# Joining the state's two products per sub-block into one 128-column product in a chunked RWKV-7 recurrence

## The chip, the cores and the metric

The kernel runs on one core of a Trainium2 chip. The metric is device time of the whole program, in microseconds (us). The core's engines are TensorE (PE, matrix products; PEld is its weight load), VectorE (DVE), ScalarE (ACT), GpSimd (POOL) and SyncE (SP, which issues most of the DMAs). Each engine works through its own list of instructions in order; semaphores tie the lists together.

## What is computed

One pre-norm residual layer over 256 tokens of width 2048. A combined input projection (2048 x 22672, float32) feeds four token mixers; their outputs are gated, projected, merged and projected once more. The mixer that matters here is RWKV-7 time mixing, with 16 heads of 64:

```python
def step(state, inp):
    r_t, w_t, k_t, v_t, a_t, b_t = inp
    sa = jnp.einsum('bhvk,bhk->bhv', state, a_t)
    state = (state * w_t[:, :, None, :] + sa[..., None] * b_t[:, :, None, :]
             + v_t[..., None] * k_t[:, :, None, :])
    return state, jnp.einsum('bhvk,bhk->bhv', state, r_t)
...
u = jnp.einsum('bsd,dn->bsn', h, w_in)
a_in, b_in, b_gate, c_qkv, c_f, c_gate, d_in, d_gate, m_logit = _split(u, IN_SIZES)
y_a = _short_conv_branch(a_in, conv_w)
y_b = _rwkv7_branch(b_in, b_gate, ...)
y_c = _fox_branch(c_qkv, c_f, c_gate, fox_bf)
y_d = _pool_branch(d_in, d_gate, pool_w, pool_scale)
...
proj = jnp.einsum('bskc,kcd->bskd', ys, w_branch)
gates = jax.nn.sigmoid(m_logit.reshape(bsz, s, N_BRANCH, d) + b_merge)
return x + jnp.einsum('bsd,de->bse', jnp.sum(gates * proj, axis=2), w_out)
```

## The kernel before

**The big products.** All weights come from HBM in float32. `chunk` (L255) makes 512 output columns for both blocks of 128 tokens. A weight tile `raw` (two slices of 128 rows) is split by ACT into a rounded part `wh` (L275) and by DVE into the rest `wl` (L276), and PE multiplies high by high and high by low (L245, the tile written is `psm`) and low by high (L249). There are three buffers of `raw`, six of `wh` and six of `wl`, so that DVE can be at most three pairs of `wl` ahead of PE. Each pair of slices gives twelve products with 512 moving columns.

**The recurrence.** It runs for two halves of eight heads (`hf`), in each for two blocks of 128 tokens (`rwkv_block`, b = 0 and 1), in each for two sub-blocks of 64 tokens (e = 0 and 1): eight sub-blocks, of which the first of each half has no state yet (`ch` = 0). A block first transposes its scaled factors into `GT` and `BK` (L499 to L503), then the Gram matrices on PE (L509), copied under a mask into `G` by DVE (L513); four transposes (L523) bring the triangles together in `MT`, a chain of 31 small multiply and reduce steps on DVE inverts them (L530, L532), four more transposes write `UF` (L538), and L540 to L555 complete it. Then, for each sub-block:

- `from_state_and_keys(0)`: four products of the state `SB` with a 66-column slice of `GT` (L571) and eight of the tokens' values with 66-column slices of `G` (L575) are added up in the PSUM tile `ps_z`; ACT copies them to `z` (L580);
- `UF` times `z` (L584), copied by ACT into the values `uv` (L585); the state's update (L590);
- `from_state_and_keys(1)`: the same twelve products with the other 66 columns, and ACT copies them to `y` (L591; `y` is the tile that rows name `e`);
- DVE takes the update over into `SB` (L597 to L600); after the second sub-block, DVE normalises `y` (L607 to L623).

There is one buffer of `ps_z`, so the second group of products can't start before `z` has been copied.

**Order.** The tile framework orders each engine's list by a simulated timeline with priorities: the weights' split first, then the recurrence, then the attention heads (L686 to L714), then the rest. So the recurrence's instructions stand among the big products of other parts of the layer, and a change in one place moves others.

Of the kernel before, what the change touches and what calls it, by code (L numbers as in the profile page):

```python
# [9 lines left out]
F32 = mybir.dt.float32  # L10
# [3 lines left out]
ALU = mybir.AluOpType  # L14
# [80 lines left out]
def kernel(  # L95
# [267 lines left out]

    Gt = rw.tile([P, NH * 2 * P + 8], F32, name="G")
    G = slots(Gt, NH)
# [112 lines left out]
    def rwkv_block(hf, b, u, prep):  # L478
# [15 lines left out]
        for p2 in range(0, NPAIR, 2):  # L494
# [16 lines left out]
            for par in range(2):  # L511
                h = 2 * p2 + par
                v.copy_predicated(out=G[:, h:h + 3:2],  # L513
                                  mask=rmask.unsqueeze(1).unsqueeze(1).to_broadcast([P, 2, 2, P]),
                                  data=gps[par].rearrange("p (h e t) -> p h e t", h=2, e=2))
# [3 lines left out]
        for q in range(4):  # L519
            e, d = q // 2, q % 2  # L520
            ds = slice(32 * d, 32 * d + 32)
            src = G[ds, :, e, ds].rearrange("p u t -> p t u").unsqueeze(2).to_broadcast([32, 32, 4, NH])
            v.transpose(out=MT[32 * q:32 * q + 32].rearrange("p t (r u) -> p t r u", u=NH), in_=src)  # L523
# [19 lines left out]
        for h in range(NH):  # L543
            for e in range(2):
                j = (h * 2 + e) * 32
                nc.tensor.matmul(tps[0:32, j:j + 32], lhsT=G[0:32, h, e, 32:64], rhs=X1[0:32, h, e, :],
                                 start=True, stop=True)
# [14 lines left out]
        for e in range(2):  # L562
# [3 lines left out]
            def from_state_and_keys(part):  # L566

                o = psum_ex("z")
                if ch:
                    for p in range(NPAIR):  # L570
                        nc.tensor.matmul(o[0:MORE, p * P:(p + 1) * P], lhsT=after(GTt, 4 * p + 2 * e + part),  # L571
                                         rhs=SB[:, p, :], start=p == 0, stop=False)
                for h in range(NH):
                    hs = slice(h * H, (h + 1) * H)
                    nc.tensor.matmul(o[0:MORE, hs], lhsT=after(Gt, 4 * h + 2 * e + part), rhs=uv[:, hs],  # L575
                                     start=ch == 0, stop=ch == 0 or h == NH - 1)
                return o[lo]


            sc.activation(out=z[lo], in_=from_state_and_keys(0), func=AF.Copy)  # L580
# [10 lines left out]
            sc.activation(out=y[ts], in_=from_state_and_keys(1), func=AF.Copy)  # L591
# [367 lines left out]
```

## Time and profile before

| | |
|---|---|
| three runs | 1418.52, 1424.03 and 1423.12 us, median 1423.12 us |
| the profiled execution | 1420.26 us, span of the trace 1418.5 us |
| PE busy | 1387.2 us (98% of the span) |
| DVE busy | 968.3 us (68%) |
| ACT busy | 712.3 us (50%) |
| DMA | 266.20 MB, 188 GB/s on average |

The span is the time from the first to the last instruction of the trace; around it lie 1.8 us of the execution's time. A product with float32 operands shows as two PE instructions in the trace (a transpose as one), and as one row in the order of the program.

### The profile page before, as it was taken

What the parts mean: (1) busy time and instruction counts of PE and PEld (TensorE: products, weight loads), DVE (VectorE), ACT (ScalarE), POOL (GpSimd) and SP (SyncE); (2) the same over time, 40 slices, a digit from 0 to 9 for tenths busy, and PEclk for the clock granted to TensorE, in tenths of its full rate; (3) what the DMA queues carried; (4) which work ended last, traced back from release to release, by engine and by line L of the source; (5) the groups of instructions that cost most, each with busy time, mean ns of one, the idle gap of its engine ahead of it and who ended that gap; (6) DMA issues with size and microseconds to landing.
All of it is one profiled execution on the core that took longest, in us unless ns stands there. A gap on an engine that the chain in (4) does not pass through costs nothing.

```text
span 1418.5 us, 20184 instructions
## 1 busy us (share of the span) xinstructions
PE 1387.2 (98%) x6961; PEld 1149.7 (81%) x6961; DVE 968.3 (68%) x1724; ACT 712.3 (50%) x1298; POOL 75.1 (5%) x149
## 2 busy tenths in 40 slices
PE   8999999999999999999999999999999999999997
PEld 6877778887788788887888888888888888888885
DVE  5558989589857979679957655565655556556654
ACT  6455744554445565554535544444444444444444
POOL 0310000011002100010000000000000000000000
PEclk9999999999999999999999999999999999999999
DMA  7876645446557655555545566666666666776664
GB/s 243 214 214 206 189 144 177 140 129 206 177 151 221 209 162 167 175 156 166 178 147 162 161 204 198 203 192 209 203 200 187 206 209 198 231 230 201 194 201 148
DMA packets 136918, 266.20 MB, mean 188 GB/s; under 512 B 11609, under 2 KB 16392, under 8 KB 136816
## 3 DMA queue, kind: packets, MB, share of 16 engines
q1 hardware_dynamic: 128448, 239.83, 55.2%
q0 software_dynamic: 7760, 24.04, 6.1%
q8 instruction: 54, 0.88, 0.3%
q10 hardware_dynamic: 608, 1.06, 0.2%
q14 instruction: 48, 0.39, 0.1%
HBM read 257.44 MB, written 2.10 MB: 183 GB/s over the span
## 4 chain that ended last, share of the span: by engine, by line
PE 79%; DVE 6%; issue 3%; DMA 2%; ACT 1%; POOL 0%; DVEq 0%; ACTq 0%; POOLq 0%
PE psm L245 47%; PE psm L249 24%; DVE wl L276 2%; DMA raw<-in_w_out_dram 1%; PE ps_z L575 1%; PE ps_r L509 1%; DMA cg<-pz 1%; DVE MT L523 1%; DVE tm L530 1%; PE ps_z L571 1%; PE ps_c L846 1%; PE ps_r L584 0%; PE ps_c L686 0%; PE ps_r L499 0%; PE ps_c L691 0%
## 5 line engine op out<-in xcount | busy, mean ns | idle before, releaser
L276 DVE TENSOR_TENSOR wl<-raw,wh 128x512 fp32r<-128x512 f32 (+1 forms) x896 | 576.6, 679 | 334.6 <-ACT wh L275 287.1
L275 ACT ACTIVATE wh<-raw 128x512 fp32r<-128x512 f32 (+1 forms) x896 | 513.5, 619 | 542.7 <-PE psm L245 319.4
L245 PE MATMUL psm<-wh,xh 128*128 128x512 f32 (+1 forms) x1440 | 564.7, 393 | 5.5 <-ACT wh L275 3.8
L245 PE MATMUL psm<-wh,xl 128*128 128x512 f32 (+1 forms) x1440 | 560.9, 391 | 0.0
L249 PE MATMUL psm<-wl,xh 128*128 128x512 f32 (+1 forms) x1440 | 411.8, 392 | 4.3 <-DVE wl L276 4.2
L245 PEld LDWEIGHTS psm<-wh,xh 128*128 128x128 f32 x1440 | 271.3, 189 | 64.3 <-ACT wh L275 7.2
L249 PEld LDWEIGHTS psm<-wl,xh 128*128 128x128 f32 x1440 | 266.5, 188 | 62.6 <-DVE wl L276 9.7
L245 PEld LDWEIGHTS psm<-wh,xl 128*128 128x128 f32 x1440 | 271.4, 189 | 52.4 <-issue 0.5
L530 DVE TENSOR_TENSOR tm<-UQ,MT 128x16 f32<-128x16 f32 (+30 forms) x124 | 52.4, 422 | 2.1
L532 DVE TENSOR_REDUCE UQ<-tm 128x8 f32<-128x16 f32 (+30 forms) x124 | 36.2, 292 | 2.3
L782 DVE SCALAR_TENSOR_TENSOR qa<-psm,rstd,row 128x512 f32<-128x512 f32 x32 | 23.9, 748 | 18.3 <-PE psm L249 18.3
L784 ACT ACTIVATE qa<-qa 128x1024 f32<-128x1024 f32 x16 | 17.0, 1061 | 37.3 <-DVE qa L782 37.3
L184 POOL DMA_DIRECT2D row<-in_b_merge_dram x16 | 8.7, 541 | 507.0 <-DVE qa L782 433.7
L523 DVE STREAM_TRANSPOSE MT<-G 32x1024 f32<-32x1024 f32 x16 | 32.0, 2001 | 0.2
L245 PE MATMUL psm<-wh,ybh 128*128 128x512 f32 x64 | 24.9, 389 | 0.0
L245 PE MATMUL psm<-wh,ych 128*128 128x512 f32 x64 | 24.9, 389 | 0.0
L245 PE MATMUL psm<-wh,ydh 128*128 128x512 f32 x64 | 24.9, 389 | 0.0
L245 PE MATMUL psm<-wh,yah 128*128 128x512 f32 x64 | 24.9, 389 | 0.0
L245 PE MATMUL psm<-wh,yal 128*128 128x512 f32 x64 | 24.9, 389 | 0.0
L245 PE MATMUL psm<-wh,ybl 128*128 128x512 f32 x64 | 24.9, 389 | 0.0
L245 PE MATMUL psm<-wh,ycl 128*128 128x512 f32 x64 | 24.9, 389 | 0.0
L245 PE MATMUL psm<-wh,ydl 128*128 128x512 f32 x64 | 24.9, 389 | 0.0
(381 smaller groups left out, 1355.5 us busy)
## 6 DMA issues: line engine op xcount, KB each, us to landing
raw<-in_w_in_dram SPq DMA_DIRECT2D x343, 512.0 KB, 4.2
raw<-in_w_branch_dram SPq DMA_DIRECT2D x64, 512.0 KB, 4.7
raw<-in_w_out_dram SPq DMA_DIRECT2D x32, 512.0 KB, 4.9
row<-in_b_merge_dram POOLq DMA_DIRECT2D x16, 256.0 KB, 4.0
raw<-in_w_in_dram SPq DMA_DIRECT2D x8, 328.0 KB, 4.5
raw<-in_w_in_dram SPq DMA_DIRECT2D x8, 312.0 KB, 3.3
cg<-pz POOLq DMA_DIRECT2D x4, 448.0 KB, 5.3
x<-in_x_dram SPq DMA_DIRECT2D x3, 512.0 KB, 8.7
```

Of the source, the lines that this page charges most:

```text
L245: nc.tensor.matmul(ps[b][:, :n], lhsT=st[:, k, b * P:(b + 1) * P], rhs=wh[:, :n], start=k == 0 and st is sth, stop=False)
L249: nc.tensor.matmul(ps[b][:, :n], lhsT=sth[:, k, b * P:(b + 1) * P], rhs=wl[:, :n], start=False, stop=k == nk - 1)
L275: sc.activation(out=h[:, :n], in_=raw[:, j, :n], func=AF.Copy)
L276: v.tensor_tensor(out=l[:, :n], in0=raw[:, j, :n], in1=h[:, :n].bitcast(F32), op=ALU.subtract)
L509: nc.tensor.matmul(gps[par][:, j * P:(j + 1) * P], lhsT=BK[:, i, par, e, :], rhs=GT[:, p2 + i, e, :], start=True, stop=True)
L523: v.transpose(out=MT[32 * q:32 * q + 32].rearrange("p t (r u) -> p t r u", u=NH), in_=src)
L530: v.tensor_tensor(out=tm[:, :, 0:n], in0=UQ[:, i:32, :].rearrange("p j c -> p c j"), in1=MT[:, i:32, i].unsqueeze(1).to_broadcast([P, 8, n ...
L532: v.tensor_reduce(out=UQ[:, i, :], in_=tm[:, :, 0:n], axis=AX.X, op=ALU.add)
L571: nc.tensor.matmul(o[0:MORE, p * P:(p + 1) * P], lhsT=after(GTt, 4 * p + 2 * e + part), rhs=SB[:, p, :], start=p == 0, stop=False)
L575: nc.tensor.matmul(o[0:MORE, hs], lhsT=after(Gt, 4 * h + 2 * e + part), rhs=uv[:, hs], start=ch == 0, stop=ch == 0 or h == NH - 1)
L782: v.scalar_tensor_tensor(out=gt[:, b, :], in0=ps[b], scalar=rstd[:, b:b + 1], in1=bm, op0=ALU.mult, op1=ALU.add)
L784: sc.activation(out=flat(gt), in_=flat(gt), func=AF.Sigmoid)
```

## The change

The state's product is made once per sub-block, with all 128 columns of `GT`: rows 0 to 63 of `ps_z` get the share of `z`, rows 64 to 127 the share of `y`. The tokens' first eight products still have 66 columns, the last two of them zero (`G` now holds 66 columns for each slot, 64 of them written). Since they no longer cover all rows, a product of two columns with weights that are all zero closes the accumulation. ACT copies the upper half into `y` behind the copy of `z`; the tokens' eight products for `y` go to the next `ps_z` alone, and DVE adds them to `y` in place of ACT's copy. For `ch` = 0 there is no state product and ACT copies as before. The masked copy into `G` becomes two copies of half the size each.

```diff
--- before.py
+++ after.py
@@ -361,8 +361,9 @@
 
         return t[:, 0:t.shape[-1] - 8].rearrange("p (u e t) -> p u e t", u=n, e=2)
 
-    Gt = rw.tile([P, NH * 2 * P + 8], F32, name="G")
-    G = slots(Gt, NH)
+
+    Gt = rw.tile([P, NH * 2 * 2 * MORE], F32, name="G")
+    G = Gt.rearrange("p (u e w t) -> p u e w t", u=NH, e=2, w=2)
     SB = rw.tile([P, NPAIR, P], F32, name="SB")
     UFt = rw.tile([MORE, NH * 2 * SUB + 8], F32, name="UF")
     UF = slots(UFt, NH)[0:64]
@@ -510,16 +511,18 @@
                                      start=True, stop=True)
             for par in range(2):
                 h = 2 * p2 + par
-                v.copy_predicated(out=G[:, h:h + 3:2],
-                                  mask=rmask.unsqueeze(1).unsqueeze(1).to_broadcast([P, 2, 2, P]),
-                                  data=gps[par].rearrange("p (h e t) -> p h e t", h=2, e=2))
+                for w in range(2):
+                    v.copy_predicated(
+                        out=G[:, h:h + 3:2, :, w, 0:SUB],
+                        mask=rmask[:, w * SUB:(w + 1) * SUB].unsqueeze(1).unsqueeze(1).to_broadcast([P, 2, 2, SUB]),
+                        data=gps[par].rearrange("p (h e w t) -> p h e w t", h=2, e=2, w=2)[:, :, :, w])
 
 
         MT = rw.tile([P, 32, 32], F32, name="MT")
         for q in range(4):
             e, d = q // 2, q % 2
             ds = slice(32 * d, 32 * d + 32)
-            src = G[ds, :, e, ds].rearrange("p u t -> p t u").unsqueeze(2).to_broadcast([32, 32, 4, NH])
+            src = G[ds, :, e, 0, ds].rearrange("p u t -> p t u").unsqueeze(2).to_broadcast([32, 32, 4, NH])
             v.transpose(out=MT[32 * q:32 * q + 32].rearrange("p t (r u) -> p t r u", u=NH), in_=src)
         gp.memset(flat(MT)[:, 0:1024:33], 1.0)
         UQ = rw.tile([P, 32, 8], F32, name="UQ")
@@ -543,7 +546,7 @@
         for h in range(NH):
             for e in range(2):
                 j = (h * 2 + e) * 32
-                nc.tensor.matmul(tps[0:32, j:j + 32], lhsT=G[0:32, h, e, 32:64], rhs=X1[0:32, h, e, :],
+                nc.tensor.matmul(tps[0:32, j:j + 32], lhsT=G[0:32, h, e, 0, 32:64], rhs=X1[0:32, h, e, :],
                                  start=True, stop=True)
         v.tensor_copy(out=X1[32:64].rearrange("p u e t -> p (u e t)"), in_=tps[0:32, :])
         tps = psum_ex("r")
@@ -563,21 +566,24 @@
             ch = 2 * b + e
             ts = slice(e * SUB, (e + 1) * SUB)
             uv = vs[:, b, :] if e == 0 else uv1
-            def from_state_and_keys(part):
-
-                o = psum_ex("z")
-                if ch:
-                    for p in range(NPAIR):
-                        nc.tensor.matmul(o[0:MORE, p * P:(p + 1) * P], lhsT=after(GTt, 4 * p + 2 * e + part),
-                                         rhs=SB[:, p, :], start=p == 0, stop=False)
+            def from_keys(o, w, fresh):
                 for h in range(NH):
                     hs = slice(h * H, (h + 1) * H)
-                    nc.tensor.matmul(o[0:MORE, hs], lhsT=after(Gt, 4 * h + 2 * e + part), rhs=uv[:, hs],
-                                     start=ch == 0, stop=ch == 0 or h == NH - 1)
-                return o[lo]
-
-
-            sc.activation(out=z[lo], in_=from_state_and_keys(0), func=AF.Copy)
+                    nc.tensor.matmul(o[0:MORE, hs], lhsT=G[:, h, e, w], rhs=uv[:, hs], start=fresh, stop=fresh)
+
+
+            zy = psum_ex("z")
+            if ch:
+                for p in range(NPAIR):
+                    nc.tensor.matmul(zy[:, p * P:(p + 1) * P], lhsT=GT[:, p, e, :], rhs=SB[:, p, :], start=p == 0,
+                                     stop=False)
+            from_keys(zy, 0, ch == 0)
+            if ch:
+
+                nc.tensor.matmul(zy[:, HALF - 2:HALF], lhsT=K("cmask")[:, 0:P], rhs=SB[:, 0, 0:2], start=False, stop=True)
+            sc.activation(out=z[lo], in_=zy[lo], func=AF.Copy)
+            if ch:
+                sc.activation(out=y[ts], in_=zy[hi], func=AF.Copy)
             ups = psum_ex("r")
             for h in range(NH):
                 hs = slice(h * H, (h + 1) * H)
@@ -588,7 +594,12 @@
                 for p in range(NPAIR):
                     pc = slice(p * P, (p + 1) * P)
                     nc.tensor.matmul(sps[:, pc], lhsT=(bk1 if e else bk0)[:, pc], rhs=uv[:, pc], start=True, stop=True)
-            sc.activation(out=y[ts], in_=from_state_and_keys(1), func=AF.Copy)
+            yk = psum_ex("z")
+            from_keys(yk, 1, True)
+            if ch:
+                v.tensor_tensor(out=y[ts], in0=yk[lo], in1=y[ts], op=ALU.add)
+            else:
+                sc.activation(out=y[ts], in_=yk[lo], func=AF.Copy)
             if ch < NSUB - 1:
                 sv = sps.rearrange("p (a d) -> p a d", d=P)
                 for rs in (lo, hi):
```

Three places of the order show what moves. The first is PE's list at the second sub-block of the first block (half 1), `ps_z` with the state `SB` and the tokens' values `e_...`, then the attention head's products (`ps_c`) and the big ones (`psm`). Before:

```order
L571 MATMUL ps_z<-SB,GT 66x128 x4
L575 MATMUL ps_z<-e_1699,G 66x64 x8
L709 MATMUL ps_c<-va,pT 128x64
L710 MATMUL ps_c<-va,pT 128x64
L711 MATMUL ps_c<-va,pT 128x64
L686 MATMUL ps_c<-cst,qa 66x128 x2
L686 MATMUL ps_c<-cst,ka 66x128 x2
L249 MATMUL psm<-wl,xh 128x512 x4
```

And now:

```order
L578 MATMUL ps_z<-SB,GT 128x128 x4
L572 MATMUL ps_z<-e_1703,G 66x64 x8
L583 MATMUL ps_z<-SB,cst 128x2
L715 MATMUL ps_c<-cst,pt 128x128 x3
L249 MATMUL psm<-wl,xh 128x512 x4
```

The four state products have 128 rows out in place of 66, the two-column product (L583) stands behind the tokens' eight, and another step of the attention head follows. The second group of four (before, eighteen rows further down) is gone.

The second place is DVE's list in the second block of half 1, at the end of the inversion (`tm`, `UQ`), where `UF` is written. `ya` and `yc` are other mixers' outputs, `wl` is the weights' split. Before:

```order
L530 TENSOR_TENSOR tm<-UQ,MT 128x256
L532 TENSOR_REDUCE UQ<-tm 128x8
L538 STREAM_TRANSPOSE UF<-UQ 32x8x4x8
L276 TENSOR_TENSOR wl<-raw,wh 128x512
L538 STREAM_TRANSPOSE UF<-UQ 32x8x4x8 x3
L276 TENSOR_TENSOR wl<-raw,wh 128x512
L310 SCALAR_TENSOR_TENSOR ya<-psm,rstd,ya 128x512 x2
L540 STREAM_TRANSPOSE X_1966<-UF 32x512
L714 SCALAR_TENSOR_TENSOR yc<-ps_c,sm,yc 128x64 x2
L312 TENSOR_TENSOR ya<-ya,sg 128x512 x2
L276 TENSOR_TENSOR wl<-raw,wh 128x512 x6
```

And now:

```order
L276 TENSOR_TENSOR wl<-raw,wh 128x512 x2
L535 TENSOR_REDUCE UQ<-tm 128x8
L310 SCALAR_TENSOR_TENSOR ya<-psm,rstd,ya 128x512 x2
L533 TENSOR_TENSOR tm<-UQ,MT 128x256
L725 SCALAR_TENSOR_TENSOR yc<-ps_c,sm,yc 128x64 x2
L312 TENSOR_TENSOR ya<-ya,sg 128x512 x2
L535 TENSOR_REDUCE UQ<-tm 128x8
L541 STREAM_TRANSPOSE UF<-UQ 32x8x4x8 x4
L276 TENSOR_TENSOR wl<-raw,wh 128x512 x2
L543 STREAM_TRANSPOSE X_1972<-UF 32x512
L276 TENSOR_TENSOR wl<-raw,wh 128x512 x6
```

The four transposes into `UF` and the six instructions on `ya` and `yc` now stand in one piece between two pairs of `wl`, where before two single `wl` stood among them.

The third place is DVE's list in the first block of half 1, from the masked copies into `G` to the start of the inversion. Before:

```order
L513 COPY_PREDICATED G<-cst,ps_r 128x2x256 x2
L523 STREAM_TRANSPOSE MT<-G 32x1024 x3
L276 TENSOR_TENSOR wl<-raw,wh 128x512
L523 STREAM_TRANSPOSE MT<-G 32x1024
L276 TENSOR_TENSOR wl<-raw,wh 128x512 x3
L530 TENSOR_TENSOR tm<-UQ,MT 128x8x2
```

And now:

```order
L515 COPY_PREDICATED G<-cst,ps_r 128x2x2x64 x4
L526 STREAM_TRANSPOSE MT<-G 32x1024 x4
L276 TENSOR_TENSOR wl<-raw,wh 128x512 x4
L533 TENSOR_TENSOR tm<-UQ,MT 128x8x2
L276 TENSOR_TENSOR wl<-raw,wh 128x512 x2
L535 TENSOR_REDUCE UQ<-tm 128x8
```

Two copies have become four, and the single `wl` among the transposes has moved behind them.

## Rows read from the trace of the kernel before

**Rows 1.** The page: busy us (share of the span) xinstructions, and PE's granted clock in 40 slices.

```profile
PE 1387.2 (98%) x6961; PEld 1149.7 (81%) x6961; DVE 968.3 (68%) x1724; ACT 712.3 (50%) x1298; POOL 75.1 (5%) x149
...
PEclk9999999999999999999999999999999999999999
```

**Rows 2.** Waits of PE: engine line <- what ended it: us in total, times, longest us.

```profile
PE psm L249 <- DVE wl L276: 4.2, 5, 2.3
PE psm L245 <- ACT wh L275: 3.8, 5, 1.3
```

**Rows 3.** Timeline of PE, a sub-block: start us, us, engine, line, out<-in, shapes, count.

```profile
262.26 0.84 PE L249 MATMUL psm<-wl,xh 128*128 128x512 f32 x3
262.94 1.05 PE L590 MATMUL ps_r<-s,pv 128*128 128x128 f32 x8
263.83 1.12 PE L575 MATMUL ps_z<-s,G 128*66 128x64 f32 x16
...
269.94 1.03 PE L571 MATMUL ps_z<-SB,GT 128*66 128x128 f32 x8
270.81 1.12 PE L575 MATMUL ps_z<-e,G 128*66 128x64 f32 x16
```

**Rows 4.** Timeline of PE, products with few moving columns.

```profile
102.15 0.38 PE L658 MATMUL ps_c<-cf,cst 128*128 128x16 f32 x2
102.38 0.72 PE L249 MATMUL psm<-wl,xh 128*128 128x512 f32 x2
...
245.00 1.19 PE L546 MATMUL ps_r<-X,G 32*32 32x32 f32 x32
246.13 0.43 PE L709 MATMUL ps_c<-va,pT 128*128 128x64 f32 x2
```

**Rows 5.** ACT's copies out of `ps_z`, line L591: ns min/median/max, first and last start.

```profile
L591 ACT ACTIVATE e<-ps_z x8: 589/590/592, 265.0 to 747.0; 64x512 f32<-64x512 f32 x8
```

**Rows 6.** DVE by line and form: busy us, mean ns, then idle us before.

```profile
L523 DVE STREAM_TRANSPOSE MT<-G 32x1024 f32<-32x1024 f32 x16 | 32.0, 2001 | 0.2
...
L513 DVE COPY_PREDICATED G<-cst,ps_r 128x512 f32<-128x512 int32 x16 | 11.9, 741 | 6.8 <-PE ps_r L509 6.1
...
L864 DVE TENSOR_TENSOR va<-psm,qa 128x512 f32<-128x512 f32 x8 | 5.5, 683 | 0.0
...
L842 DVE COPY sg<-ps_c 128x256 f32<-128x256 f32 x8 | 3.2, 412 | 1.1 <-PE ps_c L841 1.0
```

**Rows 7.** Timeline of PE, three waits: in brackets idle us and what ended it.

```profile
372.44 0.50 PE L249 MATMUL psm<-wl,xh 128*128 128x512 f32 x1 [0.66 <-DVE wl L276]
375.23 0.50 PE L249 MATMUL psm<-wl,xh 128*128 128x512 f32 x1 [2.29 <-DVE wl L276]
...
656.28 0.33 PE L704 MATMUL ps_c<-cst,pt 128*128 128x128 f32 x1 [2.37 <-ACT pt L699]
```

**Rows 8.** Timeline of DVE around the longest wait.

```profile
372.42 2.03 DVE L538 STREAM_TRANSPOSE UF<-UQ 32x256 f32<-32x256 f32 x3
374.48 0.69 DVE L276 TENSOR_TENSOR wl<-raw,wh 128x512 fp32r<-128x512 f32 x1
375.09 1.40 DVE L310 SCALAR_TENSOR_TENSOR ya<-psm,rstd,ya 128x512 f32<-128x512 f32 x2
...
377.03 0.42 DVE L714 SCALAR_TENSOR_TENSOR yc<-ps_c,sm,yc 128x64 f32<-128x64 f32 x2
377.39 1.27 DVE L312 TENSOR_TENSOR ya<-ya,sg 128x512 f32<-128x512 f32 x2
```

**Rows 9.** Stretches behind two waits: busy us (x) of PE, PEld, DVE, ACT, POOL, granted clock.

```profile
375.70:379.10 3.40, 3.24 (x9) 2.53 (x9) 3.22 (x8) 1.26 (x2) 0.00 (x0) 0.51 0.53 154
656.90:660.30 3.40, 3.40 (x17) 2.81 (x18) 3.40 (x10) 2.68 (x5) 0.00 (x0) 1.00 0.65 166
```

**Rows 10.** The page's groups of the inversion: busy us, mean ns of one.

```profile
L530 DVE TENSOR_TENSOR tm<-UQ,MT 128x16 f32<-128x16 f32 (+30 forms) x124 | 52.4, 422 | 2.1
L532 DVE TENSOR_REDUCE UQ<-tm 128x8 f32<-128x16 f32 (+30 forms) x124 | 36.2, 292 | 2.3
```

## The prediction

> **What bounds the kernel now.** I read the page first: PE is busy for 98% of the span, DVE for 68%, and the granted clock is at nine tenths or more in all 40 slices [rows 1]. So the kernel is as long as PE's list, plus the few microseconds in which PE waits. The list of PE's waits comes next: what it waits for behind the start is the weights' split, with 4.2 us for `wl` and 3.8 us for `wh` [rows 2]. PE's timeline then says where: 0.66 and 2.29 us in the second block of half 1, and 2.37 us in the last block of half 0, for an attention tile that comes late from ACT [rows 7]. DVE's timeline shows why: at 372 to 378 us it has no gap, PE's product starts within 0.1 us of the end of the `wl` that it needs, and that `wl` stood behind three transposes of 2.03 us together [rows 7, 8]. So in the four blocks DVE lags behind PE for a while, because the inversion's 248 small steps (52.4 and 36.2 us) and the transposes stand among the splits [rows 10]. The change thus has two prices: what it takes from PE's list, and what it does to DVE's lag.
>
> **PE's list.** The state products of six sub-blocks are made once in place of twice: 6 x 4 = 24 of 48 go. Four of them hold PE from 269.94 to 270.81 us, 0.87 us or 0.218 each [rows 3]; 24 are 5.2 us. Those that stay load 128 columns of weights in place of 66. The nearest row with such weights and the same 128 moving columns is the state's update: four from 262.94 to 263.83 us, 0.222 each [rows 3]; 24 x 0.004 is 0.1 us.
>
> Added are six closing products of two moving columns. The trace has none so narrow; two rows lie near. Products with 32 moving columns and 32 x 32 weights take 16 in 1.13 us, 0.07 each; one with 16 moving columns, but 128 x 128 weights, holds PE from 102.15 to 102.38 us, 0.22 with the step to the next form [rows 4]. So a product of eight times fewer moving columns than the state's costs the same where its weights are as wide: the weights set it. I take 0.22, which has the same weights: 1.3 us, with 0.4 us as the other end. The Trainium skill says so too (TensorE: Matmul & The Clock Gate, section LDWEIGHTS): the load's time goes by the columns of the stationary operand, not by its rows, 128 columns being 107 ns by its formula; for two passes that would be an estimate of 0.21 each, in agreement with the 0.22 here, and it speaks against the change, since counting moving columns alone would make the closing product nearly free.
>
> The sixteen products with the tokens per sub-block stay at 66 columns and 64 moving ones: nothing. PE's list: -5.2 + 0.1 + 1.3 = -3.8 us (-4.7 with the cheap closing product).
>
> **ACT.** Six copies to `y` go and six of the same form come, 0.59 us each [rows 5]: nothing in sum. The new one stands behind the copy of `z` and so ahead of the copy to `uv`, but that one waits for eight products (L584) of the form of L575's eight, which take 1.12 us [rows 3]; 0.59 us is hidden there. The single `ps_z` is free again only when it is done, which matters for the tokens' second products; in the order these follow the closing product by 37 big products in the first block, 8 us at 0.227 each [rows 3].
>
> **DVE.** Sixteen masked copies of 0.741 us become 32 of half the size. The nearest form is a copy of 128x256 from PSUM, 0.412 us [rows 6]: 2 x 0.412 - 0.741 = +0.08 a pair, 1.3 us in all, 0.3 us a block; if the split costs nothing, 0, and if every half cost the whole 0.741, 11.9 us (I take the copy's row, which has the size). By the fixed cost per instruction that the skill's VectorE: DVE Perf Modes gives for sources in PSUM (section on the TRN2 errata, 120 cycles at 0.96 GHz, 125 ns) it would be an estimate of 2.0 us; no row here has the split copy. Six additions of 64x512 come, at the 0.683 us of an addition out of PSUM [rows 6]: 4.1 us. The transposes that read `G` at its new stride stay at 2.0 us each [rows 6]; with none at such a stride in the trace I leave +-10%, 0.8 us a block. As DVE is idle for a third of the span, these 5.4 us cost only where PE waits on DVE: within the blocks. An addition also holds `ps_z`, but in the order the next user of that tile stands 16 or more big products, 3.6 us, behind, against about 1.5 us for the state's instructions and the addition ahead of it.
>
> **DVE's lag, the uncertain term.** The order of the whole middle has moved. At the second place shown, DVE now has in one piece between two pairs of `wl`: 1.40 (`ya`), 0.42 (`yc`), 1.27 (`ya`) and 4 x 0.68 (transposes, a third of 2.03), with one multiply and two reduces at their means about 6.8 us [rows 8, 10], where the longest such piece there was before 3.4 us. A pair of slices is twelve big products, 2.7 us on PE [rows 3], so PE runs dry. On the other hand the two `wl` on which it waited before now come ahead of this piece. At the third place the piece grows from 2 x 0.74 + 3 x 2.0 = 7.5 us to 4 x 0.41 + 4 x 2.0 = 9.6 us [rows 6], though the last transpose was only one `wl` behind before.
>
> To weigh it I added up, from each block's last Gram product on, the durations of the rows over DVE's order up to each `wl` and over PE's up to its first use, and took the largest excess of DVE over PE. Before it is 1.9, 4.9, 0.6 and 3.7 us for the four blocks, 11.1 in sum; now 2.7, 6.5, 2.7 and 4.2, 16.1. PE's real waits there are 1.3 [rows 2], 0.66 + 2.29 and 2.37 us [rows 7], 6.6 in sum, so the reckoning overstates by 11.1 / 6.6. The 5.0 us that it adds become 3.0: I take +3. Ends: it can be the whole +5.0, and the clock can add to it. Right behind the 2.29 us wait the granted clock is 0.51 for 3.4 us [rows 9], that is 1.2 in place of 2.4 GHz; half of it, 1.7 us, is lost. Behind the 2.37 us wait it stays at 1.00 [rows 9], so a wait of this length may or may not bring a slow stretch. High end: 5.0 + 2 x 1.7 = +8.4. Low end: the wait of 2.37 us for the attention tile goes, since its DVE step no longer stands right behind the transposes, and the slow stretch with it: -2.4 - 1.7 = -4.1.
>
> **Sum.** -3.8 + 3 = -0.8 us on the profiled execution's 1420.3 us: 1419.5. The runs shown have a median of 1423.12, 2.9 us above it, and the mean of all four executions is 1421.5, 1.2 us above; I add 1 us and forecast 1420.5 us, no change that can be told. What a measurement of this kernel can tell from none is about 0.5%, 7.1 us.
>
> **Rivals.**
> - *The saving comes through, and the waits shrink.* For it: PE is busy for 98%, and the last block's attention step has moved away. Against it: DVE's work grows. -3.8 - 4.1 = -7.9 us: 1413.5 us with the same +1.
> - *DVE's lag takes more than PE saves.* One mechanism, in the second block of half 1 and in both of half 0: PE does less between the Gram products and the pair behind the transposes, meets DVE sooner and waits longer; it decides once the waits there grow by more than 3.8 us, and past the 2.3 us at which one wait cost a slow stretch each adds 1.7 us. -3.8 + 8.4 = +4.6: 1426 us. Where every half copy also cost the whole 0.741 us, 3 us a block, it would be +12 more at the most, slower by over 0.5%. Against it: in the third block the reckoning before showed 0.6 us, so there is room.
> - *The merged product doesn't run as it says*: `ps_z`, with its single buffer, is held by the copy of the upper half and by DVE's addition, and PE waits for them in every sub-block with a state. 6 x (0.59 + 0.68) = 7.6 us, less 3.8: 1425 us. Against it: 37 and 16 big products stand between.
>
> **How the numbers follow.** Forecast (-4 to +3 us around the 1420.5 with its own shift) 0.54, saving through 0.20, DVE's lag 0.20, `ps_z` 0.06. The range reaches to the first rival, 1413, and past the second, 1427, and holds some 0.82. Faster by over 0.5% takes -7.1 us: about two thirds of the first rival, 0.14 with a little for the scatter of the runs. Slower by over 0.5%: of the second and third rival under a half, 0.12. Within: 0.74.
>
> **What would show it.** PE's instructions fall by 36 (48 rows for 24 products less, 12 for 6 more); the two-column product stands about 0.2 us before the next one; the half copies take some 0.41 us and the additions 0.68. PE's waits for `wl` and `wh` in the four blocks add up to about 10 us in place of 6.6. I am wrong if the closing product costs under 0.1 us, if PE waits at `ps_z`, or if the stretches with half the clock are more than two between 150 and 760 us.

## The result, and the profile after

The changed kernel takes 1436.26 us (median of six runs, 1431.95 to 1437.97) against 1422.51 us before (six runs). The ratio is 1.0094, with an interval of 1.0080 to 1.0108: 0.9% slower, 13.8 us, and outside the predicted range of 1413 to 1427.

The page of after, its span and busy times, against [rows 1]:

```profile
span 1435.2 us, 20145 instructions
PE 1394.4 (97%) x6925; PEld 1150.7 (80%) x6925; DVE 974.7 (68%) x1746; ACT 713.5 (50%) x1298; POOL 75.1 (5%) x149
```

PE issues 36 instructions fewer, as predicted, and is busy for 7.2 us more; its idle time (span less busy) went from 31.3 us to 40.8. The core's mean granted clock, after:

```profile
core 0: 1435.2 us, clock 0.992
```

And before:

```profile
core 0: 1418.5 us, clock 0.997
```

Lost to the clock over the spans are thus 0.3% of 1418.5 us, 4.3 us, and 0.8% of 1435.2 us, 11.5 us. Where the waits came in is read from four stretches of the span; the columns are PE's busy time (and instructions), then PEld, DVE, ACT and POOL, the granted clock, the DMA share and GB/s. Before:

```profile
50.00:150.00 100.00, 93.98 (x464) 77.29 (x462) 68.20 (x116) 57.55 (x107) 10.84 (x22) 1.00 0.73 210
150.00:790.00 640.00, 630.18 (x3560) 525.45 (x3560) 508.33 (x977) 330.63 (x624) 39.96 (x79) 1.00 0.57 169
790.00:850.00 60.00, 59.76 (x270) 49.14 (x269) 36.05 (x59) 30.45 (x52) 1.07 (x2) 1.00 0.63 193
850.00:1400.00 550.00, 549.49 (x2437) 453.86 (x2436) 325.46 (x511) 256.40 (x438) 10.61 (x19) 1.00 0.65 203
```

After:

```profile
50.00:150.00 100.00, 92.73 (x454) 76.95 (x453) 66.75 (x113) 56.36 (x105) 10.85 (x22) 0.98 0.74 209
150.00:790.00 640.00, 625.85 (x3472) 516.01 (x3472) 509.46 (x992) 327.13 (x616) 39.95 (x79) 0.99 0.56 167
790.00:850.00 60.00, 55.82 (x255) 45.90 (x254) 33.69 (x54) 28.12 (x48) 1.07 (x2) 0.94 0.52 158
850.00:1400.00 550.00, 550.00 (x2443) 455.54 (x2442) 323.62 (x505) 256.49 (x436) 10.61 (x19) 1.00 0.65 204
```

Width less PE's busy time is PE's idle time. In the stretch with the four blocks, 150 to 790 us, it grows from 9.8 to 14.2 us. In the 60 us behind the blocks, where nothing was changed and PE waited for 0.2 us, it is now 4.2 us, and the clock there is 0.94. That is a place that the prediction did not look at.

What the new instructions cost, on PE's timeline of after (start, us, engine, line, operation; the times of neighbouring rows overlap, since matmuls are pipelined), against [rows 3]:

```profile
271.75 1.06 PE L578 MATMUL ps_z<-SB,GT 128*128 128x128 f32 x8
272.64 1.12 PE L572 MATMUL ps_z<-e,G 128*66 128x64 f32 x16
273.60 0.34 PE L583 MATMUL ps_z<-SB,cst 128*128 128x2 f32 x2
273.79 0.53 PE L715 MATMUL ps_c<-cst,pt 128*128 128x128 f32 x3
```

Four state products step 0.89 us, 0.222 each, and the closing product 0.19: both as predicted. DVE's groups of after, with mean ns behind the busy time, against [rows 6]:

```profile
L526 DVE STREAM_TRANSPOSE MT<-G 32x1024 f32<-32x1024 f32 x16 | 34.3, 2144 | 0.2
L515 DVE COPY_PREDICATED G<-cst,ps_r 128x256 f32<-128x256 int32 x32 | 12.0, 445 | 6.3 <-PE ps_r L510 6.2
L600 DVE TENSOR_TENSOR e<-ps_z,e 64x512 f32<-64x512 f32 x6 | 4.1, 684 | 3.6 <-PE ps_z L572 3.5
```

The additions take what was forecast. A pair of half copies takes 2 x 0.445 - 0.741 = 0.15 us more than a whole one, 2.4 us in all (forecast 1.3). The transposes that read `G` at its new stride take 0.143 us more each, 2.3 us in all (forecast nothing, with +-10% left open).

PE's waits between 150 and 790 us, summed by what they wait for (us in total, times, longest us), before:

```profile
PE psm L249 <- DVE wl L276: 3.7, 4, 2.3
PE psm L245 <- ACT wh L275: 1.3, 1, 1.3
```

And after, with the two that are new:

```profile
PE psm L249 <- DVE wl L276: 3.0, 7, 0.8
PE psm L245 <- ACT wh L275: 1.7, 2, 1.2
PE ps_c L701 <- DVE UQ L535: 2.5, 1, 2.5
PE ps_z L578 <- DVE SB L609: 1.2, 1, 1.2
```

The waits for the weights' split did not grow: 5.0 us before, 4.7 after. What grew are waits of the attention head's products (`ps_c`) and one of the state's.

### The profile page after: what moved, and what is told of

Read it like the earlier page. It is cut to its first block, busy times and chain, and to the rows that moved or that the text cites. A ratio compares the mean times of both kernels' runs of the same rounds, so it can differ in the third digit from the quotient of the medians.

```text
span 1435.2 us, 20145 instructions
## 1 busy us (share of the span) xinstructions
PE 1394.4 (97%) x6925; PEld 1150.7 (80%) x6925; DVE 974.7 (68%) x1746; ACT 713.5 (50%) x1298; POOL 75.1 (5%) x149
## 4 chain that ended last, share of the span: by engine, by line
PE 79%; DVE 9%; DMA 7%; issue 3%; ACT 2%; SPq 0%; POOL 0%; DVEq 0%; ACTq 0%
PE psm L245 47%; PE psm L249 24%; DMA raw<-in_w_in_dram 5%; DVE wl L276 3%; DMA raw<-in_w_out_dram 1%; PE ps_z L572 1%; DVE tm L533 1%; PE ps_r L510 1%; ACT wh L275 1%; DVE UQ L535 1%; DVE MT L526 1%; PE ps_r L590 1%; PE ps_r L500 0%; PE ps_c L702 0%; PE ps_z L578 0%
## 5 line engine op out<-in xcount | busy, mean ns | idle before, releaser
L249 PE MATMUL psm<-wl,xh 128*128 128x512 f32 (+1 forms) x1440 | 416.7, 395 | 4.5 <-DVE wl L276 3.5
L710 ACT ACTIVATE pt<-pt,mx 128x128 f32<-128x128 f32 (+1 forms) x32 | 14.3, 448 | 24.9 <-DVE mx L708 24.8
```

Source lines behind the costliest of these rows:

```text
L249: nc.tensor.matmul(ps[b][:, :n], lhsT=sth[:, k, b * P:(b + 1) * P], rhs=wl[:, :n], start=False, stop=k == nk - 1)
```

## The wait behind the blocks

This is PE at the end of the input stage before; the last bracket is the idle time ahead of a row and who ended it:

```profile
795.47 0.60 PE L808 MATMUL ps_z<-cst,pz 128*128 128x128 f32 x4
795.83 0.48 PE L245 MATMUL psm<-wh,xl 128*128 128x512 f32 x1
...
797.98 0.61 PE L249 MATMUL psm<-wl,xh 128*128 128x512 f32 x2
798.84 0.50 PE L245 MATMUL psm<-wh,xh 128*128 128x512 f32 x1 [0.24 <-DVE pz L310]
```

And after:

```profile
806.96 0.62 PE L249 MATMUL psm<-wl,xh 128*128 128x512 f32 x2
807.42 0.60 PE L819 MATMUL ps_z<-cst,yc 128*128 128x128 f32 x4
809.43 0.66 PE L819 MATMUL ps_z<-cst,pz 128*128 128x128 f32 x4 [1.41 <-DVE ycl L823]
812.85 0.79 PE L245 MATMUL psm<-wh,xh 128*128 128x512 f32 x1 [2.76 <-DVE pz L310]
813.44 0.63 PE L245 MATMUL psm<-wh,xl 128*128 128x512 f32 x1
813.87 0.63 PE L245 MATMUL psm<-wh,xh 128*128 128x512 f32 x1
```

DVE of after in the same microseconds:

```profile
808.68 0.69 DVE L823 TENSOR_TENSOR ycl<-ps_z,ych 128x512 fp32r<-128x512 f32 x1 [2.06 <-ACT ych L822]
810.12 1.42 DVE L861 TENSOR_TENSOR pz<-ps_c,row 128x256 f32<-128x256 f32 x4 [0.75 <-PE ps_z L819]
811.46 0.68 DVE L823 TENSOR_TENSOR ydl<-ps_z,ydh 128x512 fp32r<-128x512 f32 x1
812.05 1.40 DVE L310 SCALAR_TENSOR_TENSOR pz<-psm,rstd,pz 128x512 f32<-128x512 f32 x2
```

The chain is: the last branch computes `yd` in two halves, both in the one buffer `pz`. The scaling of the second half (L861) may write `pz` only when the transposes of the first half (L819 from `pz`) have read it. Those use `ps_z`, which has one buffer, so they stand behind the transposes of `yc`, ACT's copy and DVE's subtraction of them. The gate (L310) of the second half stands behind L861, and PE's next big product needs the PSUM tile that the gate reads. Before, the transposes from `pz` are issued with 11 big products still behind them in PE's queue (795.83 to 798.6), which cover the chain. After, the recurrence's last eight products for `y` (16 PE instructions) start at 765.44 us in place of 745.82, the transposes of the branches get `ps_z` later, and the same step stands at the very end of the queue, with nothing left to cover it.

The granted clock follows the wait; the same columns as above:

```profile
811.50:818.30 6.80, 5.45 (x13) 4.31 (x14) 4.75 (x9) 2.52 (x4) 0.54 (x1) 0.52 0.20 52
818.30:821.70 3.40, 3.40 (x21) 2.89 (x19) 3.16 (x6) 2.24 (x4) 0.00 (x0) 1.00 0.72 217
596.50:603.30 6.80, 6.42 (x18) 5.07 (x19) 3.10 (x8) 2.57 (x7) 0.00 (x0) 0.53 0.65 227
```

It is 0.52, about 1.2 GHz, right behind PE's idle time at 808 to 813 us, and 1.00 again from 818.3. Big products step 0.43 us there (813.44 to 813.87) in place of 0.23. The other long stretch begins at 596 us, about a wait of 1.87 us that ends at 596.9. Added up over the trace, leaving out the last microseconds of the program, the halved stretches last 3.4 us before (one, [rows 9]) and 20.5 us after (four: at 118, 344, 596 and 811 us). PE is busy for 3.2 and 18.0 us of them; the rest is idle time, which is counted already. Half of the 14.7 us more, 7.4 us, is lost to the clock; the mean clock gives 7.2.

That is the profiled pair. The profiled execution of before is one of its quicker ones: its mean clock is 0.997, where 119 executions of before that ran beside the experiments have 0.995 on average, and after's six have 0.993. Between these averages the clock makes some 3.5 us.

## Experiments

Ratios are against the kernel before on the same chip, with 95% intervals. The kernel before had a median of 1422.1 to 1422.7 us throughout.

**1. Parts of the change, and a control.** The layout of `G` alone:

```diff
-    Gt = rw.tile([P, NH * 2 * P + 8], F32, name="G")
+    Gt = rw.tile([P, NH * 2 * 2 * MORE], F32, name="G")
-                v.copy_predicated(out=G[:, h:h + 3:2], ...)
+                for w in range(2):
+                    v.copy_predicated(out=G[:, h:h + 3:2, :, w, 0:SUB], ...)
```

> The kernel before with only the new layout of G (slots of 66 columns, half-size masked copies); both groups of state products stay. Theory 'DVE work' (each us that DVE gets more in the blocks is a us that PE waits, and then some for the clock): DVE gets 16 x 0.15 us for the copies and 16 x 0.13 us for the transposes at the new stride, 4.5 us, with nothing taken from PE: 1427 to 1433 us. Theory 'order' (the reordering moves the waits about, in no proportion to the work added): anything from 1415 to 1436. Theory 'merged product' (its own chain is what is late): no change, 1420 to 1425.

Measured: 1437.28 us, ratio 1.0108 (1.0093 to 1.0122). The layout by itself is as slow as the whole change, for some 4.7 us more of DVE's work. It has a wait of 2.3 us at 812 us, too.

The merged product and the addition without the layout (the tokens' products take two neighbouring columns along in place of zeros, so two rows of the share of `y` are not the reference's):

```diff
-    nc.tensor.matmul(o[0:MORE, hs], lhsT=G[:, h, e, w], rhs=uv[:, hs], ...)
+    nc.tensor.matmul(o[0:MORE, hs], lhsT=after(Gt, 4 * h + 2 * e + w), rhs=uv[:, hs], ...)
```

> The changed kernel with the old dense layout of G and one masked copy; the tokens' products for z reach two columns into the other slot, so that two rows of y in each sub-block get what doesn't belong to them. Theory 'DVE work': of the 8.6 us more on DVE the 4.1 us of the additions stay: some 1426 to 1430 us. Theory 'order': anything from 1415 to 1436. Theory 'merged product': as slow as the changed kernel, 1434 to 1438 us.

Measured: 1430.41 us, ratio 1.0051 (1.0034 to 1.0068). In 790 to 850 us PE idles for 4.2 us, as in after.

The state product merged, and the tokens' products for `y` summed onto the upper half of the same PSUM tile, with 64 columns of weights. Neither closing product, nor addition, nor layout is needed:

```diff
+            nc.tensor.matmul(zy[rows, hs], lhsT=G[:, h, e, part * SUB:(part + 1) * SUB], rhs=uv[:, hs],
+                             start=ch == 0, stop=ch == 0 or h == NH - 1)
+            sc.activation(out=y[ts], in_=zy[hi], func=AF.Copy)
```

> The product with the state made once, 128 columns; the tokens' products for y are added in the upper 64 rows of the same PSUM tile (64-column weights at the upper half of the array), so no closing product, no second copy, no addition on DVE, and G stays dense. PE loses 5.1 us of products, DVE and ACT get nothing more. Theory 'DVE work': faster than before, 1415 to 1419 us. Theory 'order': 1412 to 1430. Theory 'merged product': slower than before, since its chain stays. If 64-column weights cost a switch of the array's mode, it shows as steps over 0.12 us between those products.

Measured: 1422.33 us, ratio 1.0000 (0.9988 to 1.0012). PE has 48 instructions fewer and yet gains nothing; a wait of 2.77 us for DVE's L310 stands at 801.4 us here too. And the 64-column weights do have a price, not between those products but on the way into them and out. The state products, the eight products behind them and the next ones, before:

```profile
269.94 1.03 PE L571 MATMUL ps_z<-SB,GT 128*66 128x128 f32 x8
270.81 1.12 PE L575 MATMUL ps_z<-e,G 128*66 128x64 f32 x16
271.77 0.39 PE L709 MATMUL ps_c<-va,pT 128*128 128x64 f32 x2
271.99 0.39 PE L710 MATMUL ps_c<-va,pT 128*128 128x64 f32 x2
```

And in this kernel:

```profile
272.26 1.05 PE L577 MATMUL ps_z<-SB,GT 128*128 128x128 f32 x8
273.24 1.15 PE L571 MATMUL ps_z<-e,G 128*64 128x64 f32 x16
274.32 0.43 PE L710 MATMUL ps_c<-va,pT 128*128 128x64 f32 x2
274.59 0.39 PE L711 MATMUL ps_c<-va,pT 128*128 128x64 f32 x2
```

From the first row to the fourth it is 2.33 us in place of 2.05: 0.28 us more, of which 0.02 are the state's wider weights. The trace has 25 such stretches of products with 64-column weights (some groups of eight are split), an estimate of 6.5 us. That takes up the 5.1 us that the merged product saves.

A control that was meant only to make the planner choose another order:

```diff
+        tiny = rw.tile([P, 1], F32, name="tiny")
+        v.tensor_copy(out=tiny, in_=ones1)
```

> The kernel before with one more copy of one column on DVE per block (4 in all, under 0.1 us each): nothing in work, but the order of the middle moves. Theory 'order': the time moves by several us, either way. Theories 'DVE work' and 'merged product': 1420 to 1424 us, no change.

Measured: 1422.37 us, ratio 0.9998 (0.9984 to 1.0012). The four copies all ran at 39 us, outside the blocks, at 0.15 us each, and in the trace every other instruction of every engine stands in the order of before. So this control moved nothing: it shows that the time repeats (0.9998), and says nothing on what a new order costs.

**2. The buffer of the last branch.** One line, in after, in the kernel summed in PSUM, in before and in the merged kernel with dense `G`:

```diff
-        yd = wk.tile([P, NB, HALF], F32, name="pz")
+        yd = wk.tile([P, NB, HALF], F32, name=("pz", "va")[hf])
```

> After, with the second half of the last branch's yd in the buffer va instead of pz, so that its scaling needn't wait for the transposes of the first half. In after TensorE idles 4.2 us at 809 to 813 us behind that chain, and the clock is halved for 6.8 us from 811.5 us, which loses 3.4 us more. If that chain is where a good half of the loss lies, the two go and the time is 1436 - 7 = about 1429 us. If the wait only shows lateness that is then paid elsewhere (DVE is late whatever buffer is free), it stays within 2 us of 1436.

> The kernel with y summed in PSUM (state product once, dense G), with the same second buffer for yd. It had one wait of 2.8 us there and 1.7 us lost by a halved clock after it. If these go, 1422.3 - 4.5 = about 1418 us, ahead of the kernel before; if the lateness is paid elsewhere, 1422.

> Before with the second half of yd in va. Before shows only 0.2 us of wait there, so the buffer gives nothing: 1422 us, and what the kernel with y summed in PSUM and two buffers gained (1418.9) is due to the sum in PSUM once its lateness has a way out. Rival: the buffer itself is worth 3 us whatever the recurrence does: 1419.

> The merged state product with dense G (its tokens' products take their neighbours' columns along instead of zeros, so two rows of y are not the reference's), closing product and DVE's addition as in after, with two buffers for yd. With one buffer 1430.4, with 4.2 us of wait and 3.4 us lost by the clock at 800 us. If the chain at pz was all that the merged product cost, 1430.4 - 7.6 = 1423; if DVE's addition costs beyond it, 1426 or more.

After with it: 1427.61 us, ratio 1.0041 (1.0027 to 1.0054), 8.6 us less than after by the medians (7.5 by the two ratios), where 7 were expected. Every engine's order is that of after up to 784 us; only what stands behind that is moved. In the place of the wait:

```profile
790.00:850.00 60.00, 60.00 (x286) 49.81 (x285) 38.13 (x60) 31.07 (x52) 1.08 (x2) 1.00 0.59 181
```

PE has no idle time left there and the clock is 1.00. Before with it: 1422.18 us, 0.9993 (0.9983 to 1.0004), nothing, as there was nothing to take away. Merged with dense `G`: 1424.38 us, 1.0011 (0.9999 to 1.0023), 6.0 us less than without. Summed in PSUM: **1418.91 us, 0.9975 (0.9964 to 0.9986)**, faster than both kernels by more than its interval.

**3. The layout taken apart.** Only the copies divided, `G` dense; and the layout with undivided copies, which takes neighbouring heads for a copy so that all its slots have one stride:

```diff
+                for w in range(2):
+                    ws = slice(w * SUB, (w + 1) * SUB)
+                    v.copy_predicated(out=G[:, h:h + 3:2, :, ws], ...)
```

```diff
+                    nc.tensor.matmul(gps[i][:, j * P:(j + 1) * P], lhsT=BK[:, i, par, e, :], rhs=GT[:, p2 + i, e, :], ...)
+                h = 2 * (p2 + i)
+                v.copy_predicated(out=G[:, h:h + 2, :, :, 0:SUB].rearrange("p h e w t -> p (h e) w t"), ...)
```

> Before (dense G, old products), each masked copy into G divided into two halves: 2 x 0.445 - 0.741 = 0.15 us more for each of 16, 2.4 us more on DVE. The layout with both parts (copies 2.4 us, transposes 2.3 us) cost 14.6 us, 3 us for each us of DVE. If DVE's work there is what counts, whatever kind: about 1422.6 + 7 = 1430 us. If DVE's work costs what it takes, 1425. If the transposes' stride is what counts, 1423.

> Before with G's slots of 66 columns, but each masked copy undivided (the two heads of a copy are neighbours, so that its slots have one stride). What is left of the layout is the transposes from G at 2.14 us instead of 2.00, 2.3 us in all, and the wider weights, 0.1 us. If DVE's work is what counts, whatever kind: about 1430 us; if it costs what it takes, 1425; if the divided copies are what counts, 1423.

Divided copies: 1424.39 us, 1.0015 (1.0003 to 1.0027): 2.3 us for 16 x 0.14 us of work, as much as the work takes, though the order moves here too. Undivided with slots: 1430.63 us, 1.0063 (1.0050 to 1.0076), 8.5 us for 2.3 us of work. That brought two changes along, so the neighbours were made alone with dense `G`, and the same work was put on the chain without slots:

```diff
+            one = MT[32 * q:32 * q + 32, 0, 0:1]
+            v.tensor_copy(out=one, in_=one)
```

> Before (dense G) with the heads of a masked copy made neighbours, as in e8 and e11, and nothing else. If that assignment brought nothing along: 1422. If it is what e8 lost beyond its work, 1428 (8.5 us less the 2.3 us of the transposes).

> Before with a copy of one column (0.154 us in e4) behind each of the 16 transposes from G: 2.4 us of DVE's work where the slots put 2.3 us, without the slots. If work on that chain is paid several times over: about 1430; if it costs what it takes, 1424.5; if it is hidden, 1422.

Neighbours alone: 1425.19 us, 1.0019 (1.0007 to 1.0031). They add no work and lose 3.0 us; what is left to differ is the order of the Gram products and the one that the planner then chooses. In 450 to 620 us PE idles for 5.9 us (170.00 less 164.06), 1.8 before. With the divided copies alone it idles there for 5.85 us too, so this is not the neighbours' own mark. Before, and with neighbours:

```profile
450.00:620.00 170.00, 168.19 (x928) 139.47 (x927) 138.96 (x257) 94.93 (x179) 10.35 (x21) 1.00 0.59 176
450.00:620.00 170.00, 164.06 (x893) 134.14 (x892) 133.74 (x251) 89.59 (x170) 9.09 (x18) 1.00 0.56 167
```

The work without slots, 16 copies of

```profile
L525 DVE COPY MT<-MT 32x1 f32<-32x1 f32 x16 | 2.3, 144 | 0.4
```

give 1424.66 us, 1.0024 (1.0010 to 1.0038): 2.4 us for 2.3 us of work. So my theory that work on this chain is paid three times over fell. That the time equals the work is not shown to be more than chance: the order moves here as well, and in this trace PE idles for 2.8 us behind the blocks, with the clock at 0.97:

```profile
790.00:850.00 60.00, 57.23 (x254) 47.03 (x253) 34.20 (x56) 29.00 (x49) 1.07 (x2) 0.97 0.57 177
```

The layout with the second buffer, and the same with the eight heads' slots side by side:

```diff
-    G = Gt.rearrange("p (u e w t) -> p u e w t", u=NH, e=2, w=2)
+    G = Gt.rearrange("p (e w u t) -> p u e w t", u=NH, e=2, w=2)
```

> The layout alone (slots of 66 columns, divided copies; 1437.3) with two buffers for yd. It had 2.3 us of wait at 812 us and 1.7 us lost by the clock behind it: 1433 if these go and nothing comes in their place, 1429 if as much is saved as in after (8.6 us).

> As e15, with the slots of a half and a sub-block side by side for the eight heads, so that the transposes step by 264 bytes from head to head instead of 1056 (1024 in before). If the step sets their 2.14 us, they change (2.00 or less), DVE's chain is 2.3 us shorter and the time falls below that of e15 by 2 us or more; if it is the tile's size or something else, they stay at 2.14 us and the time at that of e15.

Measured: 1434.01 us, 1.0084 (1.0065 to 1.0104), and 1429.92 us, 1.0060 (1.0043 to 1.0078). The order of instructions is the same on every engine. The transposes in the first,

```profile
L525 DVE STREAM_TRANSPOSE MT<-G 32x1024 f32<-32x1024 f32 x16 | 34.3, 2141 | 0.2
```

and in the second:

```profile
L525 DVE STREAM_TRANSPOSE MT<-G 32x1024 f32<-32x1024 f32 x16 | 32.5, 2032 | 0.2
```

The step is what lengthens them. But 4.1 us for 1.75 us of work is not certain (3.4 by the ratios), since the two intervals overlap, and the same line in after with two buffers gave nothing:

> e5 (after with two buffers for yd, 1427.6) with the slots of the eight heads side by side, in the same order of instructions: its transposes take 2.03 us instead of 2.14, 1.75 us less on DVE. If each us there costs 2.3, as from e15 to e16, 1427.6 - 4.1 = 1423.5; if it costs what it takes, 1426; if hidden here, 1427.6.

Measured: 1427.95 us, 1.0032 (1.0019 to 1.0044), with the transposes at 2.05 us. In the kernel summed in PSUM, `G`'s blocks side by side (a step of 512 bytes in place of 1024):

> e6 (y summed in PSUM, dense G, two buffers; 1418.9) with G's blocks of the eight heads side by side, so that its transposes step by 512 bytes instead of 1024. If a shorter step is quicker, they fall below 2.00 us and the time by 1 to 3 us; if 1024 is as good as 512, 1418.9.

Measured: 1418.62 us, 0.9980 (0.9969 to 0.9990), and the transposes at 2.006 us, as before. The step of 512 bytes gives nothing; the gain over before is there a second time, in the same order of instructions.

After with undivided copies and two buffers:

> After with undivided masked copies (the two heads of a copy are neighbours) and two buffers for yd. Divided copies cost 2.1 us alone, so 1427.6 - 2 = about 1425.5 if the parts add up; the slots' stride alone cost 8.5 us, which then stays. If the parts overlap (one lateness paid once), 1427.6 stays.

Measured: 1430.71 us, 1.0050 (1.0034 to 1.0066), 3.1 us above the one with divided copies by the medians, although DVE has 2 us less to do (the two intervals overlap). That the order with neighbouring heads eats it is likely, but not shown apart. Its row for 450 to 620 us has 8.3 us of idle time, where after with divided copies and two buffers has 5.9 (170.00 less 164.10):

```profile
450.00:620.00 170.00, 161.74 (x867) 129.38 (x867) 133.39 (x248) 90.87 (x170) 7.76 (x16) 1.00 0.57 167
```

**4. The addition's place.** Before, with DVE in place of ACT copying `y` behind the first sub-block:

```diff
+            if ch:
+                v.tensor_copy(out=y[ts], in_=from_state_and_keys(1))
```

> Before, with the six copies of y behind the first sub-block on DVE instead of ACT: 6 x about 0.68 us on DVE for 6 x 0.59 on ACT, at the place where after has its additions. If DVE's work at this place costs what it takes, 1422 + 4 = 1426; if it is hidden beside TensorE, 1422; if the lateness it makes is multiplied as with the slots, 1430 or more.

Measured: 1428.37 us, 1.0039 (1.0023 to 1.0054), 5.7 us for this work:

```profile
L592 DVE COPY e<-ps_z 64x512 f32<-64x512 f32 x6 | 4.1, 684 | 3.2 <-PE ps_z L575 3.1
```

More than it takes, and with it the wait behind the blocks is there again, in a kernel whose products are those of before (their order differs from 289 us on):

```profile
802.51 0.50 PE L245 MATMUL psm<-wh,xh 128*128 128x512 f32 x1 [2.53 <-DVE pz L310]
```

## Why the prediction was wrong

**PE's list** was right as far as steps show it: state products at 0.222, closing product at 0.19 (0.22 forecast), so -4.0 in place of -3.8. The Trainium skill's page TensorE: Matmul & The Clock Gate, section LDWEIGHTS, by which the weights' columns set the price, gave an estimate of 0.21; the trace agrees. The merged product summed in PSUM is 3.3 us faster than before with two buffers on either side by the medians (2.6 by the ratios, whose intervals touch). That is not its list: the 64-column weights take up what it saves. PE's idle time in its two profiles is 29.8 and 27.8 us, 31.3 before; what makes the rest of the gain isn't shown.

**ACT at nothing** was right: PE shows no wait for the new copy. The rival of `ps_z` held by copy and addition in the recurrence did not come either: PE's one new wait at a state product, 1.2 us at 646 us, is for `SB`.

**DVE's sum** was mis-sized: 2.4 + 2.3 + 4.1 = 8.8 us, not 5.4. For the copies the nearest row (a copy of that size, 0.412) was too low; the fixed cost that the Trainium skill's VectorE: DVE Perf Modes states (section The TRN2 errata), from which the prediction worked out an estimate of 2.0 us in all, came nearer to the 2.4 measured. For the transposes no row had the stride, and I took the middle of +-10%, where it came out at +7%.

**DVE's lag** is the step that failed. I reckoned the lag only "from each block's last Gram product on" and took DVE's work to cost "only where PE waits on DVE: within the blocks", so that what stands behind the blocks got no term at all, without a reason. There the runs show the largest single loss. Inside the blocks PE's idle time grew by 4.3 us, near the +3, but that is luck: the waits for `wl` and `wh` were to grow to about 10 us from 6.6 (of which 2.37 were a wait for an attention tile), and went from 5.0 to 4.7; other waits came in their place. (The longest earlier piece of DVE's list was 3.8 us by its durations rather than 3.4, with the 0.69 us of L540; no term hangs on it.) With the clock inside the blocks (10.2 us of halved stretches in place of 3.4) it is some 7.5 us, near the high end of "+8.4". What the lag left out:

- The wait behind the blocks, 4.0 us of idle time and 2.7 us of halved clock (half of the 5.45 us that PE is busy in that stretch). The second buffer took both away and gave back 8.6 us (7.5 by the ratios), in a kernel whose order is the same up to 784 us. It is a buffer that before had just enough big products behind it.
- The clock, 7.4 us in this execution, 2.7 of them at that wait. In the blocks I allowed two stretches more, and no more came there: two (344 and 596 us, the second twice as long) where before had one. The others are one at 118 us ahead of the blocks and the one behind them.

So in the profiled execution: -4.0 (list) + 9.5 (idle time) + 7.4 (clock) = 12.9 of the 16.7 us by which the span grew. The 3.8 us that remain are in PE's busy time, whose ends are modelled; I can't place them.

The rival that I priced at 1426 us, DVE's lag taking more than PE saves, has the right sign. Its place ("in the second block of half 1 and in both of half 0") is only part of it, the waits that it meant did not grow, and its price was 10 us too low. None of the three signs of being wrong came: the closing product took 0.19 us, PE did not wait for `ps_z` in the recurrence, and between 150 and 760 us there are two halved stretches, not more. They watched the places that had been priced.

What of the rest stands, in kernels that all have two buffers: before 1422.2; merged with dense `G`, closing product and addition 1424.4; after, with the layout added, 1427.6. The addition and closing product in place of the sum in PSUM cost 1424.4 - 1418.9 = 5.5 us, for 1.3 us on PE and 4.1 on DVE, although the sum in PSUM pays for its 64-column weights. The layout costs another 3.2 us there, where its work is 4.7 us. What stays open is why the layout costs 11.8 us on the kernel before (1434.0) and 3.2 on the merged one. Its work alone doesn't explain it: work of 2.3 us on the same chain cost 2.4. In its profile PE idles for 38.1 us (31.3 before) and the mean clock is 0.993 (0.997), so most of it is waits and clock; what sets them off isn't shown. The order may be it, since neighbouring heads cost 3.0 us with no work at all, but no run changes the order alone: every kernel that gives DVE more work than before has another order too, and the control kept the old one.

## What to carry to other kernels

Where a planner sets the order, look not only at what waits in the stage that is changed, but at what runs beside it and behind it: a stage that is covered by just enough work before has no wait in its profile, and loses its cover when the work ahead ends later. Look there for single buffers on a chain over three engines; a second buffer that gives nothing before (1422.2) can be what lets a change pay (1418.9). Where PE is busy for 98%, count a wait of 2 us with a halved clock that may stand behind it (here after waits of 1.9 and 2.5 us, but not after the 2.37 us of [rows 7]). Here a sum in PSUM beat an addition on the engine that splits the weights, by 5.5 us. And see in the trace whether a control changed what it was made to change: the one here left the order as it was.

## What the runs showed of the hardware

- A transpose of 32x1024 on DVE takes 2.00 us where the inner step of its source is 1024 bytes (2.006 at 512), 2.14 at 1056 and 2.03 to 2.05 at 264. The note on 16-byte lines in the Trainium skill's SBUF — State Buffer (section Door 1: The DMA port swizzle) says that each access that crosses to a new line pays a penalty. Each of these steps does so at every element, so the note gives no reason for a difference. The measurement decides: here there is one, of up to 7%.
- Products with 64 columns of weights into the upper or the lower 64 rows of a PSUM tile, summed onto a product of all 128 rows, have a price where PE goes from wider weights to them and back: by the rows of the kernel summed in PSUM against those of before, where they have 66 columns, 0.26 us for a stretch of eight. Of that, 0.12 lie in the stretch itself (1.08 us from its start to the next form, 0.96 before).
